# A decoder trunk on one core: the maximum of a weight strip over the partitions, by GpSimd's all-reduce or by two transfers through DRAM and a VectorE maximum

## The chip, the cores and the metric

The kernel runs on one core of one Trainium2 chip. The metric is the device time of one execution in microseconds. The kernel before was run three times, and its median is the number to compare with.

A core has a matrix engine (TensorE, PE in the profile, with its weight loads as PEld), VectorE (DVE), ScalarE (ACT), GpSimd (POOL) and a sync engine (SP), which in this kernel does nothing but issue transfers. Each engine works through its own queue in order. An instruction whose inputs are not there yet holds up all that stands behind it in that queue, and nothing in the others.

## What is computed

The reference is one inference step of a small hybrid decoder: 1,024 prompt tokens with 16 meta tokens ahead of them, and 8 single new tokens of running sequences, 1,048 columns in all, with a model width of 1,024. Cut to what matters:

```python
for i in range(2):
    h = rms_norm(x, norm_mix_pre[i])
    m = ssd_mixer(h, ...) if i == 0 else rglru_mixer(h, ...)
    x = x + rms_norm(m, norm_mix_post[i])
    h = rms_norm(x, norm_ffn_pre[i])
    r = relu(h @ ffn_w1[i])                                  # 1024 -> 4096
    x = x + rms_norm((r * r) @ ffn_w2[i], norm_ffn_post[i])  # 4096 -> 1024
```

Inputs and weights are float32. The mixers have products with weights too: 1024 to 6176 and 2048 to 1024 in the first (SSD), 1024 to 2048 and 1024 to 1024 in the second (LRU).

## The kernel before

**Weights in strips.** Every product with weights is made from float16 parts: a float32 operand is scaled by a power of two and split into a high and a low part, and three products (high by high, high by low, low by high) are summed in PSUM. The weights come in strips of [128, 8 x 256] float32, 1 MB each. `wlane` (line 399) walks through the list of strips that `setup` made (lines 216 to 232). For each it starts the load of the next one on SP (`load_strip`, line 257, into one of two buffers `ws`), and converts the present one (`wconv`, line 285) into float16 tiles `wh`, of which there are five. The steps of a conversion are:

- the largest magnitude in each partition, [128, 1], called `rm`: a VectorE reduction for most kinds of strip (for the ffn's second product by way of `r4`, `r4s`), an ACT sum of magnitudes as a bound for the SSD strips (kind a), or a number that was found earlier (`gmx`, kind s);
- `strip_scale` (line 262): the maximum of `rm` over the 128 partitions, on every partition (`wgb`), by `partition_all_reduce` on GpSimd; then tiny VectorE steps, in the trace `qw`, `pw`, `sw`, `winv`, that make a power of two of it (`pow2`, line 245);
- for strips of kinds H and S, `quarter` and `sums` (lines 340 and 349): three quarters of the strip are split into `wp` by ACT and VectorE, then four GpSimd instructions add and subtract quarters within the strip (`ws<-ws`), for Winograd's form of the product (seven quarter products for eight);
- `split` (line 271): the high parts by ACT, the low parts by VectorE, into `wh`. When the last is done, the strip's buffer is free for a load.

There are 109 strips with a scale of their own: 33 in the SSD layer (of which one is a narrow one for dt), 32 in each of the two ffns, 12 in the LRU layer. Two more all-reduces are made once each: of the gains at the start (`gb`, line 191) and of bounds in the LRU layer (`gx`, line 1487).

**The ffn.** `ffn` (line 1226) makes four blocks, each with four strips of the first product and four of the second. In the blocks after the first (and, for the second product, in the first three) a unit of 256 rows by a chunk of some 350 tokens is computed by `unit` (line 1350): matmuls into four PSUM tiles, and VectorE and ACT steps that empty them into a tile `z`. GpSimd makes the sums of quarters of the right operand: for the squares in `t_sums` (line 1319, tiles `z` and `r`), and for the ffn's input, while the first block's second product runs, in `input_sums` (line 1332, tiles `f`). ACT and VectorE then split these into float16 (`TT`, `HT`, `H`). The tiles `z`, `r` and `f` share four buffers.

**Other transfers near the change.** In the SSD layer SP loads cumulative sums spread over the partitions for each chunk of 128 tokens (`L<-csd`, line 1017, two buffers), and sends one small row per group through DRAM and back, spread over all partitions (`bcd<-row`, line 1090, and `bc<-bcd`, line 1093).

**What sets the order.** The conversion of strips, the norms and the sums are generators; `tick` (line 127) takes one step of each between products. This sets a priority. The framework then orders the instructions of each engine by priority and by when it reckons their inputs to be there, so an engine's order is not just that of the program: the `qw` of a strip can stand ahead of the `wh` of the strip before. It also sets the semaphores that every instruction waits for. Nearly all instructions are issued through one helper, so that the profile gives them line 89 (or 92, inside a block with a forced order); they are told apart by the names of their tiles.

Tiny tiles come from the pool `tiny` (line 156) with three buffers per name, unless said otherwise.

Of the kernel before, what the change touches and what calls it, by code (L numbers as in the profile page):

```python
# [21 lines left out]
P = 128  # L22
# [31 lines left out]
def cols(c):  # L54
    """The columns of a chunk of tokens."""
    return slice(c * CW, c * CW + WC[c])


class Carve:
    """Small float32 tiles cut from larger ones."""  # L60
# [17 lines left out]
class Queue:  # L78
    """An engine; while hold is set its instructions are issued in program order, and later ones behind them."""
# [38 lines left out]
class Body:  # L118
# [7 lines left out]
    # ------------------------------------------------------- order of work  # L126
    def tick(self):
        """One step of every piece of work that runs beside the matrix products."""
        for lane in list(self.lanes):
            if next(lane, self) is self:  # L130
                self.lanes.remove(lane)
# [5 lines left out]
    def tab(self, *args, **kw):  # L137
        """An activation whose function needs a table set: these stay in program order."""
        if self.last_tab is None or self.nc.scalar.hold:
            self.last_tab = self.nc.scalar.activation(*args, **kw)  # L140
        else:
            with self.tc.issue_after(self.last_tab.ins):
                self.last_tab = self.nc.scalar.activation(*args, **kw)
# [8 lines left out]
    # ---------------------------------------------------------------- setup  # L152
    def setup(self):
        nc, tc, ctx = self.nc, self.tc, self.ctx
        self.const = ctx.enter_context(tc.tile_pool(name="const", bufs=1))
        self.tiny = ctx.enter_context(tc.tile_pool(name="tiny", bufs=3))
# [25 lines left out]
        # pre-norm gains and group-norm gains scaled by a power of two so that hi/lo fit float16  # L182
# [13 lines left out]
        # the inputs of the ffn leave room for sums of four  # L196
# [13 lines left out]
        self.csd = self.dram.tile([288, P], F32, name="csd")  # L210
        self.bcd = [self.dram.tile([8, 2, P], F32, name=f"bcd{i}") for i in range(2)]
# [33 lines left out]
    def pow2(self, b, n, pool, tag):  # L245
        """p = the power of two at or below b; s = 2^14 / p."""
# [9 lines left out]
    # -------------------------------------------------------------- weights  # L256
# [5 lines left out]
    def strip_scale(self, gmax):  # L262
        nc, ty = self.nc, self.tiny
        gb = ty.tile([P, 1], F32, tag="wgb", name="wgb")
        nc.gpsimd.partition_all_reduce(gb, gmax, P, RED.absmax)
        s, p = self.pow2(gb, 1, ty, "w")
        inv = ty.tile([P, 1], F32, tag="winv", name="winv", bufs=8)
        nc.vector.tensor_scalar(inv, p, 2.0 ** -14, None, op0=OP.mult)
        return s, inv, gb

    def split(self, w, st, s, parts):
        """w = float16 hi and lo parts of st * s, s [P, parts] by contiguous column ranges."""
# [12 lines left out]
    def wconv(self, st, kind, cols=SW):  # L285
        """A strip of weights as float16 hi and lo parts [P, 2, KT, cols], the factor that undoes its scaling and,
        for kinds h and H, the factor of its hidden units. Kind a takes a bound from the sums of the magnitudes, kind s
        one that kind g found before; kinds 2 and S carry the factors of the hidden rows. Kinds H and S are for the
        products by Winograd's form: with the quarters that are used as they are."""
# [50 lines left out]
    def quarter(self, s, inv):  # L340
        """Scales that leave room for sums of four."""
# [7 lines left out]
    def sums(self, wp, st, s, npair, parts):  # L349
        """Steps: the quarters of a strip [K tiles, M] that are used as they are, A11, A12, A22 (A ij: m tile i, k  # L350
        tiles of parity j), as float16 parts in wp; then the sums of Winograd's form in the room of the strip. Only
        the first npair pairs of k tiles."""
# [20 lines left out]
    def product(self, ps, i, w, B, T, npair):  # L373
        """ps = one of the seven products of quarters over the first pairs of k tiles, three passes of the float16
        parts; open for the products of the other pairs where there are any."""
# [14 lines left out]
    def quadrant(self, w, B, npair, i, l):  # L390
        """The operands of m tile i by half l of the tokens over the other pairs."""
# [26 lines left out]
    def hidden_scale(self, wmax, inv):  # L418
        """The factors of one strip's hidden units: t = 2^7, or 2^6 where the squares are summed, / (power of two at or
        below the bound on the values before the square, the norm of the input times that of a column); returns  # L420
        t / (scales of the product); 1 / t^2 goes to rj."""
# [21 lines left out]
    def summed(self, b, s):  # L443
        """Whether the hidden units of a strip of block b enter the second product by Winograd's form."""
        return b < 3 and s < NSUM
# [6 lines left out]
    def bundle(self, ps, w, m, act, c, kts=range(KT), first=True, last=True):  # L452
        """ps += sum over k of w[k, m tile]^T act[k, chunk c], three passes of the float16 parts."""
# [14 lines left out]
    def new_u(self):  # L468
        """Float16 parts of the normed input by chunk and k tile."""
# [4 lines left out]
    def u_rows(self, U, c):  # L474
        """The bytes of chunk c of U as float32 rows."""
        return U[:, c].bitcast(F32).rearrange("p k s c -> p k (s c)")

    # ---------------------------------------------------------------- norms
    def rstd(self, sumsq, n, pool, w):
        """1 / sqrt(mean + eps) on every partition, from per-partition sums of squares."""  # L480
# [17 lines left out]
    def normed(self, x, ss, i, hi, lo, pool):  # L498
        """Steps: the pre-norm i of a chunk (its k tiles in x), as float16 parts in hi and lo [P, KT, n]."""
# [15 lines left out]
    def boundary(self, m, ss, xc, piece, ipost, xdst, ipre, U, pool):  # L515
        """Steps: x + norm(m) for a piece of a chunk to xdst; then its pre-norm."""
# [37 lines left out]
    def last_phase(self, ws, act, ipost, xsrc, xdst, ipre, evac, pre=None, split0=None):  # L554
        """The last product before a norm, chunk by chunk; the norms of a chunk run beside the next one."""
# [47 lines left out]
    def first_phase(self, strips, act, evac):  # L603
        """Products of the first strips after a norm: chunk 2 of the input comes last."""
# [15 lines left out]
    # ------------------------------------------------------------------ SSD  # L620
# [67 lines left out]
    def start_x(self, c):  # L688
        """A chunk of the input, in the room of later rows: its k tiles, and room left over."""
# [25 lines left out]
    def start_norm(self, U, c, x, sq, ufs):  # L715
        """Steps: the first pre-norm of a chunk."""
# [29 lines left out]
    def start(self, U):  # L746
        """The first pre-norm beside the first products, issued in this order."""
# [20 lines left out]
    def dt_phase(self, U, dts, dtt, w):  # L768
        """Step sizes, decays and their cumulative sums, tokens on partitions: columns (tile, head); tiles 0-7
        are the chunks of the prompt, 8 the meta tokens, 9 the sample tokens."""  # L770
# [31 lines left out]
        # the sums again, tokens along the rows, in DRAM, from where they are spread over the partitions  # L802
# [22 lines left out]
        # sample tokens  # L825
# [3 lines left out]
        # head rows by sample, then spread over the partitions of the features  # L829
# [13 lines left out]
    def softplus(self, out, x, pool, n, parts=1):  # L843
        """max(x, 0) + log1p(exp(-|x|)), the logarithm by the series of 2 artanh(e / (2 + e)); by parts of the
        columns that don't wait for each other."""
# [23 lines left out]
    def evac_ext(self, pre, ps, c, inv, bias=0.0):  # L869
        """A chunk of projected columns into the layout of the convolution: 8 x (3 state + 1), 3 zeros, tokens."""  # L870
# [10 lines left out]
    def conv_tile(self, pre, out, w4, b1, cvo):  # L881
        """Depthwise convolution of width 4; the last three columns of each sequence go to cvo [P, 27]."""
# [16 lines left out]
    def proj_x(self, g, start=False):  # L899
        """Projection and convolution of the x, B and C columns of a group."""  # L900
# [84 lines left out]
    def ssd_group(self, g):  # L985
# [26 lines left out]
        def spread(i):  # L1012
            """The cumulative sums of a chunk's tokens on every partition."""
# [68 lines left out]
        def sample_bc():  # L1082
            """B and C of the sample tokens, by way of DRAM, on every partition."""
# [22 lines left out]
        def sample_b(b2):  # L1106
            """Two sample tokens: h += x B and y = h C, B and C spread over the partitions."""
# [45 lines left out]
    def group_norm(self, g):  # L1153
        """Steps: gate, norm within the group, float16 parts."""
# [25 lines left out]
    def half_a(self):  # L1180
        """The first half of the output projection, kept in DRAM by chunks."""
# [43 lines left out]
    # ------------------------------------------------------------------ FFN  # L1225
    def ffn(self, l):
# [8 lines left out]
        for b in range(4):  # L1235
# [3 lines left out]
            def square(c, s, r):  # L1239
                """The squares of r (m tile, half of the tokens) as float16 parts, and their sums."""  # L1240
# [78 lines left out]
    def t_sums(self, f, t1, t234):  # L1319
        """Steps: the sums of quarters of the right operand for Winograd's form, in their room in f (B jl: k tiles of  # L1320
        parity j, half l of a chunk's tokens, the last half first): T1 = B12 - B11, T2 = B22 - T1, T3 = B22 - B12,
        T4 = B21 - T2, and their float16 parts."""
# [9 lines left out]
    def input_sums(self, U, TT, fp):  # L1332
        """Steps: the sums of quarters of the input, T1 in the room of B12 and the others in TT."""
# [16 lines left out]
    def unit(self, w, BT, c, npair, fp):  # L1350
        """Two m tiles by a chunk, [C12, C11, C22, C21] (C il: m tile i, half l of the tokens, the last half first), the
        first pairs of k tiles by Winograd's form: seven products of quarters."""
# [27 lines left out]
    # ------------------------------------------------------------------ LRU  # L1380
    def lru(self):
# [99 lines left out]
        # a bound on |h gate|: (32.3 max|x| + max|h0|) (norm of u times that of a column of weights + max|b|)  # L1481
# [74 lines left out]
def _strips(w, ns):  # L1556
    """[K, N] as [ns, 128, (K / 128) * (N / ns)], each strip contiguous per partition."""
# [4 lines left out]
def _fm(x):  # L1562
    """[..., n * 128] as [128, n, ...]"""
# [95 lines left out]
```

## Time and profile before

| | |
|---|---|
| runs | 2830.25, 2836.51, 2837.24 us |
| median | 2836.51 us |
| profiled execution, span | 2836.7 us |
| VectorE, ACT busy | 2110.1 us (74%), 1322.6 us (47%) |
| mean granted TensorE clock | 0.968 |
| all-reduces of strips on GpSimd | 109 (100 + 5 + 4 in three groups) |

A line of a group of instructions gives line, engine, operation, the tiles (written <- read), the shapes and the count; then busy time in us and the mean in ns of one; then the idle time of that engine just before these instructions and what ended most of it ("issue" means nothing that the profile shows). A timeline row gives start and duration in us, the instruction and how many were merged, and in brackets the engine's idle time before the first of them. SPq, POOLq are an engine's sequencer, that waits and issues transfers. A row of DMA issues ends with the size in KB and the median time from issue to landing in us. The SSD layer fills the time to about 900 us, its last product and norm reach to about 1060, the first ffn to about 1690, the LRU layer to about 2110, the second ffn to the end.

### The profile page before, as it was taken

The page shows a single profiled execution, that of the slowest core. Times are in us where ns is not written, and L with a number is a line of the kernel's source. Part 1 is how long each engine was busy: PE and PEld are TensorE (multiplying, and loading weights), DVE is VectorE, ACT ScalarE, POOL GpSimd, SP SyncE. Part 2 cuts the span into 40 slices and gives each one's busy share as a digit, 9 for nine tenths or more (in the row PEclk, how much of TensorE's full clock was granted, in tenths as well). Part 3 has the DMA queues.
Part 4 walks back from the last instruction along what each step waited for, and adds up shares of the span by engine and source line. Part 5 has one row for each costly group of instructions (what it writes and reads, how often), then busy time and mean ns, then how long its engine had stood idle before and what let it go on. Part 6 is the DMA issues. An engine that isn't in the chain of part 4 may idle for free. (4 is left out here: it accounts for less than half of the span.)

```text
span 2836.7 us, 56933 instructions
## 1 busy us (share of the span) xinstructions
PE 2583.1 (91%) x23209; PEld 2060.6 (73%) x23209; DVE 2110.1 (74%) x5043; ACT 1322.6 (47%) x2148; POOL 691.4 (24%) x972
## 2 busy tenths in 40 slices
PE   4999999999999999789989999979999779989998
PEld 2666666666666667789989976646667779989976
DVE  4889778977873685568778788787685667878776
ACT  4655455545544354344253344658564335253352
POOL 2222111212212024442232201123014452231301
PEclk9999999999999999889999999989999989999999
DMA  3232233223345320101122123110220101111122
GB/s 123 99 119 90 87 107 115 102 88 108 113 159 187 117 106 31 46 31 46 61 72 79 46 110 113 63 62 33 89 108 31 46 31 46 47 45 53 54 73 95
DMA packets 52758, 229.15 MB, mean 81 GB/s; under 512 B 9056, under 2 KB 18416, under 8 KB 31632
## 3 DMA queue, kind: packets, MB, share of 16 engines
q1 hardware_dynamic: 46112, 190.81, 19.1%
q0 software_dynamic: 6384, 34.71, 3.1%
q8 instruction: 181, 2.97, 0.4%
q14 instruction: 81, 0.66, 0.1%
HBM read 186.28 MB, written 39.22 MB: 79 GB/s over the span
## 5 line engine op out<-in xcount | busy, mean ns | idle before, releaser
L89 PEld LDWEIGHTS <-wh 128*128 128x128 f16 x17040 | 1504.0, 99 | 503.7 <-issue 54.7
L89 PE MATMUL mm<-U,wh 128*128 128x350 f16 (+3 forms) x7056 | 989.4, 297 | 20.7 <-ACT rr L89 13.2
L89 PE MATMUL mm<-H,wh 128*128 128x175 f16 (+5 forms) x5664 | 557.7, 253 | 35.3 <-DVE z L89 30.4
L89 PEld LDWEIGHTS <-wp 128*128 128x128 f16 x3888 | 311.0, 99 | 87.6 <-issue 60.5
L89 POOL TENSOR_TENSOR ws<-ws 128x256 f32<-128x256 f32 (+1 forms) x192 | 205.2, 1069 | 328.6 <-DVE wp L89 214.4
L89 DVE TENSOR_TENSOR z<-z,mm 128x175 f32<-128x175 f32 (+3 forms) x648 | 228.4, 370 | 29.2 <-ACT z L89 22.0
L89 POOL PARTITION_ALL_REDUCE wgb<-rm x100 | 55.5, 555 | 656.6 <-issue 338.4
L89 PE MATMUL mm<-U,wp 128*128 128x175 f16 (+1 forms) x1728 | 154.8, 245 | 55.2 <-DVE z L89 55.1
L89 PE MATMUL mm<-TT,wh 128*128 128x175 f16 (+1 forms) x1728 | 167.0, 248 | 10.2 <-ACT TT L89 9.3
L89 ACT ACTIVATE z<-z,ti 128x700 f32<-128x700 f32 (+1 forms) x72 | 63.0, 875 | 183.5 <-DVE z L89 183.5
L89 DVE SCALAR_TENSOR_TENSOR wh<-ws,sw,wh 128x1024 f16<-128x1024 f32 x94 | 122.0, 1320 | 28.3 <-ACT wh L89 28.3
L89 DVE TENSOR_SCALAR qw<-wgb 128x1 f32<-128x1 f32 x103 | 15.5, 150 | 167.3 <-POOL wgb L89 167.1
L89 DVE SCALAR_TENSOR_TENSOR wh<-ws,s,wh 128x256 f16<-128x256 f32 x256 | 114.7, 490 | 11.1 <-ACT wh L89 11.1
L89 DVE TENSOR_REDUCE rm<-ws 128x1 f32<-128x2048 f32 x40 | 91.3, 2281 | 31.2 <-DMA ws<-w 26.7
L89 PE MATMUL mm<-H,wp 128*128 128x175 f16 (+1 forms) x864 | 90.5, 241 | 25.5 <-DVE z L89 23.1
L89 DVE TENSOR_TENSOR ss<-ss,sqt 128x350 f32<-128x350 f32 (+3 forms) x154 | 75.9, 500 | 41.8 <-ACT sqt L89 41.1
L89 ACT ACTIVATE wh<-ws,s 128x512 f16<-128x512 f32 x128 | 83.0, 710 | 48.0 <-POOL ws L89 23.2
L89 DVE SCALAR_TENSOR_TENSOR conv<-pre,ssmall,conv 128x1072 f32<-128x1072 f32 x78 | 103.8, 1330 | 0.1
L89 ACT ACTIVATE wh<-ws,sw 128x2048 f16<-128x2048 f32 x47 | 93.7, 1993 | 14.5 <-DVE sw L89 11.7
L89 DVE TENSOR_SCALAR L<-L,ncs 128x128 f32<-128x128 f32 (+1 forms) x288 | 90.6, 357 | 13.2 <-DMA L<-csd 13.2
L89 DVE TENSOR_TENSOR H<-z,H 128x175 f16<-128x175 f32 (+5 forms) x120 | 81.2, 694 | 23.6 <-ACT H L89 19.5
L89 ACT ACTIVATE pre<-mm,undo 128x8 f32<-128x8 f32 (+1 forms) x104 | 46.5, 474 | 110.7 <-PE mm L89 110.7
(279 smaller groups left out, 4176.9 us busy)
## 6 DMA issues: line engine op xcount, KB each, us to landing
ws<-w SPq DMA_DIRECT2D x64, 1024.0 KB, 4.9
ws<-w_ssd_in SPq DMA_DIRECT2D x24, 1024.0 KB, 5.4
L<-csd SPq DMA_DIRECT2D x64, 256.0 KB, 3.2
ws<-w_lru_in SPq DMA_DIRECT2D x12, 1024.0 KB, 4.9
xd<-xc POOLq DMA_DIRECT2D x6, 1400.0 KB, 5.5
xc<-xd SPq DMA_DIRECT2D x6, 1400.0 KB, 6.0
h<-ssd_h SPq DMA_DIRECT2D x8, 1024.0 KB, 4.9
bc<-bcd SPq DMA_DIRECT2D x8, 1024.0 KB, 4.8
```

What stands on the lines that cost most here:

```text
L89: r = f(*args, **kw)
```

## The change

`strip_scale` no longer uses GpSimd. The 128 maxima are written to a small DRAM tile (one of four in turn) by SP; SP then reads this tile as a row of 128 numbers onto each of the 128 partitions (the tile `wrow`, one buffer), and VectorE takes the maximum of the row. The pool `tiny` has two buffers per name instead of three. The rest of the diff takes out docstrings and comments; the two other all-reduces stay.

```diff
-        self.tiny = ctx.enter_context(tc.tile_pool(name="tiny", bufs=3))
+        self.tiny = ctx.enter_context(tc.tile_pool(name="tiny", bufs=2))
...
         self.csd = self.dram.tile([288, P], F32, name="csd")
+        self.mxd = [self.dram.tile([P, 1], F32, name=f"mxd{i}") for i in range(4)]
+        self.nmax = 0
...
     def strip_scale(self, gmax):
         nc, ty = self.nc, self.tiny
+        d = self.mxd[self.nmax % 4]
+        self.nmax += 1
+        nc.sync.dma_start(d, gmax)
+        row = ty.tile([P, P], F32, tag="wrow", name="wrow", bufs=1)
+        nc.sync.dma_start(row, d.rearrange("p o -> o p").to_broadcast([P, P]))
         gb = ty.tile([P, 1], F32, tag="wgb", name="wgb")
-        nc.gpsimd.partition_all_reduce(gb, gmax, P, RED.absmax)
+        nc.vector.tensor_reduce(gb, row, axis=AX.X, op=OP.max)
         s, p = self.pow2(gb, 1, ty, "w")
```

## The prediction

> **What bounds the kernel now.** I read the page first, then TensorE's groups, then the stages one by one, and then what TensorE waits for.
>
> ```profile
> span 2836.7 us, 56933 instructions
> PE 2583.1 (91%) x23209; PEld 2060.6 (73%) x23209; DVE 2110.1 (74%) x5043; ACT 1322.6 (47%) x2148; POOL 691.4 (24%) x972
> ```
>
> The profiled execution takes 2836.7 us, the median of the runs is 2836.51, so sums made on the span need no correction. TensorE is busy 91%: only its idle time, 254 us, and a slower clock can be won. On the busy row GpSimd (POOL) looks harmless with 24%.
>
> ```profile
> L89 PE MATMUL mm<-H,wh 128*128 128x175 f16 (+5 forms) x5664 | 557.7, 253 | 35.3 <-DVE z L89 30.4 <-DVE H L89 2.8 <-DVE sw L89 1.5
> L89 PE MATMUL mm<-U,wp 128*128 128x175 f16 (+1 forms) x1728 | 154.8, 245 | 55.2 <-DVE z L89 55.1
> L89 PE MATMUL mm<-H,wp 128*128 128x175 f16 (+1 forms) x864 | 90.5, 241 | 25.5 <-DVE z L89 23.1 <-DVE iq L89 1.8 <-DVE sq L89 0.5
> ```
>
> These three groups are the ffn's Winograd products; 116 us of idle time stand before them, nearly all ended by VectorE's z, the emptying of PSUM. VectorE itself is idle a quarter of the time, so the question is what holds z up. By stage (columns: PE, PEld, DVE, ACT and POOL busy, granted clock, DMA share, GB/s):
>
> ```profile
> 100.00:900.00 800.00, 762.51 (x5074) 533.41 (x5073) 632.16 (x1729) 407.20 (x620) 169.71 (x280) 0.98 0.32 113
> 1060.00:1150.00 90.00, 82.72 (x820) 69.98 (x818) 51.59 (x127) 40.00 (x82) 37.81 (x59) 0.96 0.10 36
> 1150.00:1300.00 150.00, 119.09 (x1357) 116.05 (x1355) 95.78 (x240) 62.33 (x103) 67.89 (x94) 0.87 0.10 36
> 1300.00:1690.00 390.00, 362.57 (x4473) 347.73 (x4471) 313.36 (x774) 156.30 (x268) 88.02 (x104) 0.98 0.20 73
> 2110.00:2220.00 110.00, 103.12 (x959) 82.79 (x958) 63.93 (x153) 51.31 (x103) 43.74 (x70) 0.97 0.09 30
> 2220.00:2340.00 120.00, 90.21 (x1046) 87.13 (x1044) 73.68 (x183) 44.69 (x73) 58.72 (x79) 0.87 0.10 36
> 2340.00:2740.00 400.00, 369.83 (x4669) 362.20 (x4667) 312.27 (x794) 164.36 (x288) 95.73 (x118) 0.98 0.15 54
> ```
>
> The loss sits in the ffn: six stages with 132 us of TensorE idle (stretch less PE busy), worst at 1150 to 1300 and 2220 to 2340. Those two have the lowest clock as well. Now the engines around one large gap; first GpSimd, then TensorE, then VectorE:
>
> ```profile
> 2484.50 5.38 POOL L89 TENSOR_TENSOR ws<-ws 128x512 f32<-128x512 f32 x4 [9.19 <-issue]
> 2496.07 0.41 POOL L89 PARTITION_ALL_REDUCE wgb<-rm  x1 [6.19 <-issue]
> 2503.60 4.00 POOL L89 TENSOR_TENSOR z<-z 128x175 f32<-128x175 f32 x8 [7.12 <-DVE wp L89]
> ```
> ```profile
> 2497.46 1.08 PE L89 MATMUL mm<-U,wp 128*128 128x175 f16 x12 [1.58 <-DVE z L89]
> 2510.39 1.90 PE L89 MATMUL mm<-U,wp 128*128 128x174 f16 x12 [6.07 <-DVE z L89]
> ```
> ```profile
> 2485.97 2.29 DVE L89 TENSOR_REDUCE rm<-ws 128x1 f32<-128x2048 f32 x1 [0.94 <-DMA ws<-w]
> 2496.51 0.15 DVE L89 TENSOR_SCALAR qw<-wgb 128x1 f32<-128x1 f32 x1 [4.58 <-POOL wgb L89]
> ```
>
> The strip's maxima (rm) are there at 2488.26, and the all-reduce itself takes 0.41 us. But GpSimd stands still for 6.19 us before it, having ended its sums at 2489.88, and for 7.12 us after it. Of the 63 places in this trace where the all-reduce follows a TENSOR_TENSOR directly, and the 63 the other way round, these are the ones with the least idle time:
>
> ```profile
> 1069.58 0.41 POOL L89 PARTITION_ALL_REDUCE wgb<-rm  x1 [5.74 <-issue]
> 1251.08 4.18 POOL L89 TENSOR_TENSOR z<-z 128x175 f32<-128x175 f32 x8 [6.69 <-DVE wh L89]
> ```
>
> Never less, while the eight sums of the second row ran without a gap among them. I call this the swap, some 13 us a pair; it is counted in no busy time. It costs twice. VectorE, whose queue is in order, stands at qw for 4.58 us, and TensorE loses 1.58. Then GpSimd's sums z come late, the ACT and VectorE steps behind them too, and TensorE loses 6.07.
>
> ```profile
> 2504.30:2509.50 5.20, 0.02 (x1) 0.00 (x0) 2.46 (x5) 2.67 (x7) 3.30 (x7) 1.00 0.43 176
> 2509.50:2516.30 6.80, 5.91 (x42) 5.91 (x42) 5.38 (x13) 2.05 (x5) 4.82 (x6) 0.50 0.01 4
> ```
>
> After the gap the granted clock is 0.50 for 6.8 us: a long gap is paid a second time, by 3.4 us here.
>
> **What is removed.** 109 all-reduces in the strips (two others, gb and gx, stay) and with them nearly all swaps: the swap lies between the two kinds of operation, and only the elementwise kind is left.
>
> ```profile
> L89 POOL PARTITION_ALL_REDUCE wgb<-rm x6 | 2.5, 411 | 35.9 <-issue 30.1 <-DVE z L89 5.9
> L89 DVE TENSOR_SCALAR qw<-wgb 128x1 f32<-128x1 f32 x20 | 3.1, 154 | 56.2 <-POOL wgb L89 56.2
> ```
>
> The first row is the stretch 1150 to 1300: six all-reduces with 35.9 us of standstill before them; at 6.7 at least for the way back another 40, so that GpSimd's 67.89 us of work and 76 us of swaps fill the 150. There GpSimd is the bound behind z. Without swaps it has half the stretch free. The second row is 2340 to 2740: VectorE stands 56.2 us before 20 strips, 2.8 each.
>
> **What is added.** Per strip a write of 128 x 4 bytes, a wait for its landing in SP's queue, a broadcast read of 64 KB, and a VectorE maximum of 128 elements. No such pair of transfers for a strip is in the trace; the nearest is the row that the SSD stage sends through DRAM and back (bcd, bc), then single small transfers:
>
> ```profile
> 128.64 0.34 SPq L1090 DMA_DIRECT2D bcd<-row  x1
> 132.22 0.35 SPq L907 DMA_DIRECT2D cst<-ssd_cst  x1
> 132.66 0.38 SPq L1093 DMA_DIRECT2D bc<-bcd  x1
> ```
> ```profile
> 201.70 0.30 SPq L1090 DMA_DIRECT2D bcd<-row  x1
> 203.55 0.33 SPq L1093 DMA_DIRECT2D bc<-bcd  x1
> ```
> ```profile
> ws<-w SPq DMA_DIRECT2D x64, 1024.0 KB, 4.9
> ws<-w_dt SPq DMA_DIRECT2D x1, 128.0 KB, 2.1
> lru_h_o<-lhout POOLq DMA_DIRECT2D x1, 36.0 KB, 2.0
> ```
> ```profile
> L89 DVE TENSOR_REDUCE rm<-ws 128x1 f32<-128x2048 f32 x40 | 91.3, 2281 | 31.2 <-DMA ws<-w 26.7 <-DMA ws<-w_lru_out 2.5 <-DMA ws<-w_lru_in 1.8
> L89 DVE TENSOR_REDUCE r<-ws 128x2 f32<-128x1024 f32 x64 | 76.1, 1210 | 13.3 <-DMA ws<-w 13.3
> ```
>
> Write to read issue: 1.85 us at 201.70, 4.02 at 128.64; I take 1.85, since the first had another transfer's issue between. Read: 2.1 as for 128 KB. Maximum: (2281 - 1210) / 1024 = 1.05 ns an element, so 139 + 134 = 273 ns. Sum 4.2 us from rm to the strip's maximum. Bounds: 4.0 (two transfers at the 2.0 of the smallest) and 4.02 + 4.9 + 2.1 + 0.3 = 11.3, when a strip's load of 1 MB is in the queue ahead of the read. The old way took 8.2 us at 2488.26 (to 2496.48), and only 0.5 where no swap is needed. The Trainium skill (DMA: Bandwidth & Descriptors, Specifications) speaks against the write: under 512 B a transfer is done as read-modify-write. No row here has pieces of 4 bytes; the 288-byte pieces of lhout landed in 2.0 us. By an estimate from that page's shortest HBM round trip, 0.8 us (its section on latency), the rule would add at most 64 x 0.8 = 51 us over the ffn's strips.
>
> Two more effects. VectorE gets 109 x 0.27 = 30 us of work; in the ffn stages it is idle at least a fifth of the time, so I cost it at nothing there; without that cover it is 64 x 0.27 = 17 us. The tiny tiles go from three buffers to two, also at nothing: a strip's scale is read within the strip, and the next one but one has no place to be loaded (two buffers for strips) before the first is split; if that cover fails, a strip's scale waits about a strip, and the end is as in the second rival.
>
> SP's queue is new on the path. What stands in it:
>
> ```profile
> SPq L259 <- DVE wh L89: 1659.7, 97, 66.2
> ```
>
> 97 strip loads waited there for the split of an older strip, 17 us each. So SP is mostly free when rm comes, and the write goes at once; but behind the read's wait (1.85 us) stand L's loads in the SSD stage and the loads of x at the ends of the layers, and behind both VectorE.
>
> **The sum.** (a) 1150 to 1300 and 2220 to 2340: idle 30.9 + 29.8, half clock 0.13 x 270 = 35, together 96; GpSimd gets half its time back; 70% goes, since its real work, and ACT's and VectorE's steps behind it, still come in bursts: -67. (b) 1300 to 1690 and 2340 to 2740: idle 27.4 + 30.2, clock 0.02 x 790 = 16, together 73; half goes, as VectorE's wait falls from 2.8 us but not to zero: -37. (How far it falls hangs on the order of VectorE's queue, which the framework makes anew. It does not keep the order of the program: it may lay other work into the 4.2 us, or none.) (c) 1060 to 1150 and 2110 to 2220: 14 idle and 7 clock, little of it behind strips: -4. (d) The start: the first two strips' transfers queue behind the inputs, but the next gap shrinks:
>
> ```profile
> 34.47 0.41 POOL L92 PARTITION_ALL_REDUCE wgb<-rm  x1 [5.79 <-issue]
> 41.66 6.68 POOL L92 TENSOR_TENSOR ss<-ss,sq 128x350 f32<-128x350 f32 x7 [6.78 <-issue]
> ```
>
> 6.78 us of that swap stand before sums that TensorE waits for; against it up to 7 us for the first strip: -4. (e) SSD stage: VectorE is 79% busy and gets 24 x 0.27 = 6.5 us, SP's waits come on top, some swaps go: +3. (f) New waits at the maximum, 50 strips of 0.15 us past what TensorE tolerates: +8. Sum -101, so 2736. What is late next is z behind ACT and TensorE's own pace.
>
> **Rivals.** First, nothing is won: the standstill belongs to GpSimd's sums and would stand before them anyway, or VectorE's own work is next at once. For it: VectorE is 78% busy in (b). Against: sums follow sums without a gap, and (a) has VectorE at 64%. Time 2836, within 0.3% (8.5 us, about what a measurement of this kernel tells from no change).
>
> Second, slower: the read of the maxima lands behind a 1 MB load in SP's queue. The place is qw: VectorE, in order, stands there, and z behind it. TensorE tolerates 3.0 us of this (4.58 less the 1.58 it lost). A wait of 5.5 gives a gap of 2.5, and at least 1.7 more by the clock, in 64 strips: 269; less the (a) of 67 it is +202, 3039. It decides from a wait of 3.0 + 67 / 64 = 4.0 us. For it: 11.3 us is possible by rows. Against: loads go out only after a split, and the read needs only 2 us.
>
> Third, dear transfers: the op was cheap (0.41) and two transfers take 3.8 us more; if the swaps were hidden anyway and all of this showed in 64 strips, 243 us more, 3080. The Trainium skill (GPSIMD Engine Reference, 4.1 Engine selection) is on its side: reduce along partitions on GpSimd. The rows with 6.19 and 7.12 us around 0.41 speak against.
>
> Fourth, nearly everything goes: 190 us of (a) to (c) less the 50 that no swap explains, and the start: under 2690.
>
> **Numbers.** Forecast 2736 with 0.77 in 2690 to 2805 (low: 90% of (a), 75% of (b), 10 at the start; high: 40% of (a), nothing of (b)); 0.04 between that and 2828; no change 0.05; second rival 0.04; third 0.02; fourth 0.08. Faster by over 0.3% 0.89, same 0.05, slower 0.06.
>
> **What would show it.** In the changed profile: GpSimd's sums without 6 us before them; the 1150 to 1300 stretch shorter, its clock near 1; VectorE's idle before qw or the new maximum under 1 us a strip; write to read about 1.9 us. Wrong: over 3 us of idle time before the maximum, z still late with GpSimd free, or new waits at L in the SSD stage.

## The result: 3309 us, slower by a sixth

| | median of the runs | lowest to highest |
|---|---|---|
| before | 2833.55 us (4 runs: the three above and one more) | 2830.25 to 2837.24 |
| changed | 3308.69 us (4 runs) | 3303.52 to 3313.22 |

The ratio is 1.167, with a 95% interval of 1.165 to 1.169. The profiled execution of the changed kernel has a span of 3301.8 us, 465.1 more than before. First the busy row of its page:

```profile
PE 2693.6 (82%) x23209; PEld 2146.5 (65%) x23209; DVE 2125.7 (64%) x5152; ACT 1317.6 (40%) x2148; POOL 649.3 (20%) x863
```

No engine has much more to do: VectorE 16 us, GpSimd 42 less. TensorE is idle for 608 us instead of 254, and its own 2693.6 us are 110 more for the same 23,209 matmuls, with a mean granted clock of 0.913 where it was 0.968. So work waits. To see where, I cut the span at the places where TensorE has done as many matmuls as at the stage borders of the prediction. The columns are those of the prediction's stage rows:

```profile
108.90:985.10 876.20, 785.81 (x5075) 545.89 (x5073) 653.10 (x1796) 414.15 (x631) 158.61 (x256) 0.95 0.35 104
1281.60:1448.50 166.90, 118.90 (x1357) 115.52 (x1355) 96.31 (x251) 62.46 (x106) 61.48 (x82) 0.87 0.10 35
1448.50:1948.10 499.60, 392.46 (x4473) 379.53 (x4472) 306.97 (x765) 149.37 (x259) 79.14 (x84) 0.88 0.16 55
1948.10:2439.90 491.80, 406.86 (x2505) 261.57 (x2504) 343.17 (x579) 257.25 (x380) 68.72 (x73) 0.92 0.25 74
2672.60:3202.50 529.90, 400.70 (x4670) 393.41 (x4668) 313.32 (x802) 164.46 (x286) 85.27 (x97) 0.87 0.13 41
```

The third and fifth rows, stage (b) of the prediction, took 790 us before and take 1029.5 now: half of the loss. The SSD stage (first row) loses 76 and the LRU layer (fourth row) 72; a table further down has all stages. What TensorE waits for (us in total, times, longest), its two largest waits now and its largest before:

```profile
PE mm L89 <- DVE z L89: 225.2, 71, 9.0
PE mm L89 <- DVE pw L89: 88.8, 18, 6.4
```
```profile
PE mm L89 <- DVE z L89: 113.2, 70, 6.2
```

It hardly ever waits for a strip's parts: for `wh` less than 4 us in the whole run. Both z, the emptying of PSUM, and pw stand on VectorE, and there mostly behind one instruction, the new maximum. Its group, the DMA issues of the two transfers (count, KB, median us from issue to landing), and SP's waits (us in total, times, longest), for a strip's load and between the two transfers:

```profile
L89 DVE TENSOR_REDUCE wgb<-wrow 128x1 f32<-128x128 f32 x103 | 29.3, 284 | 710.6 <-DMA wrow<-mxd 710.6
```
```profile
wrow<-mxd SPq DMA_DIRECT2D x109, 64.0 KB, 4.9
mxd<-rm SPq DMA_DIRECT2D x105, 0.5 KB, 8.3
```
```profile
SPq L261 <- DVE wh L89: 905.9, 88, 29.4
SPq L271 <- DMA mxd<-rm: 749.9, 95, 14.1
```

The maximum itself takes 284 ns, as priced at 273. But VectorE stands 710.6 us in front of 103 of them, 6.9 each, because the write of 512 bytes lands after 8.3 us and the read, which goes only then, after 4.9 more. (These are medians of the landings that the profile can place, about a quarter of them. By the issues of all strips it is 8.4 us from write to read and 5.0 from the read to the maximum.) One strip of the second ffn, first SP's queue, then three VectorE rows, then TensorE:

```profile
3017.66 0.33 SPq L261 DMA_DIRECT2D ws<-w  x1
3025.68 0.32 SPq L269 DMA_DIRECT2D mxd<-rm  x1
3034.69 0.32 SPq L271 DMA_DIRECT2D wrow<-mxd  x1
3047.57 0.33 SPq L261 DMA_DIRECT2D ws<-w  x1
```
```profile
3023.37 2.29 DVE L89 TENSOR_REDUCE rm<-ws 128x1 f32<-128x2048 f32 x1 [2.05 <-DMA ws<-w]
...
3039.37 0.29 DVE L89 TENSOR_REDUCE wgb<-wrow 128x1 f32<-128x128 f32 x1 [10.57 <-DMA wrow<-mxd]
...
3046.94 0.48 DVE L89 SCALAR_TENSOR_TENSOR wh<-ws,s,wh 128x256 f16<-128x256 f32 x1
```
```profile
3040.56 1.06 PE L89 MATMUL mm<-H,wh 128*128 128x175 f16 x6 [6.41 <-DVE pw L89]
```

Read this as a loop. The load issued at 3017.66 lands 5.71 us later, its row maxima take 2.29, the route through DRAM 13.71 (3025.66 to 3039.37), and 8.20 after that the next load goes. That load was waiting for a buffer, and the buffer for the last low part of the strip before (the row at 3046.94), and that work stands in VectorE's queue behind the wait for the row. The four steps add up to 29.91 us a strip, and nothing of one overlaps another. TensorE stands 6.41 us beside it, since z waits behind the maximum.

### The profile page after: what moved, and what is told of

The parts are those of the page before. It is cut to its first block, busy times and chain, and to the rows that moved or that the text cites. A ratio compares the mean times of both kernels' runs of the same rounds, so it can differ in the third digit from the quotient of the medians.

```text
span 3301.8 us, 57041 instructions
## 1 busy us (share of the span) xinstructions
PE 2693.6 (82%) x23209; PEld 2146.5 (65%) x23209; DVE 2125.7 (64%) x5152; ACT 1317.6 (40%) x2148; POOL 649.3 (20%) x863
## 5 line engine op out<-in xcount | busy, mean ns | idle before, releaser
L89 PEld LDWEIGHTS <-wh 128*128 128x128 f16 x17040 | 1566.5, 102 | 676.5 <-issue 116.2
L89 PE MATMUL mm<-U,wh 128*128 128x350 f16 (+3 forms) x7056 | 1016.1, 301 | 97.3 <-DVE z L89 24.8
L89 PE MATMUL mm<-H,wh 128*128 128x175 f16 (+5 forms) x5664 | 585.8, 261 | 99.5 <-DVE pw L89 61.7
L89 DVE TENSOR_REDUCE wgb<-wrow 128x1 f32<-128x128 f32 x103 | 29.3, 284 | 710.6 <-DMA wrow<-mxd 710.6
L89 PEld LDWEIGHTS <-wp 128*128 128x128 f16 x3888 | 325.2, 102 | 185.8 <-issue 183.5
L89 PE MATMUL mm<-TT,wh 128*128 128x175 f16 (+1 forms) x1728 | 178.7, 259 | 0.0
L89 ACT ACTIVATE wp<-ws,sq 128x512 f16<-128x512 f32 x72 | 48.5, 711 | 156.0 <-issue 63.5
L89 ACT ACTIVATE wp<-ws,s 128x128 f16<-128x128 f32 x144 | 48.2, 389 | 152.3 <-issue 86.2
L89 ACT ACTIVATE H<-z 128x700 f16<-128x700 f32 (+1 forms) x96 | 64.7, 674 | 102.3 <-POOL z L89 100.7
L89 PE MATMUL mm<-Y,wh 128*128 128x350 f16 (+1 forms) x576 | 93.9, 326 | 10.1 <-ACT Y L89 7.3
```

The source lines that it names most:

```text
L89: r = f(*args, **kw)
```

## The experiments

The main theory (A): the price is how the bytes lie in DRAM. 128 pieces of 4 bytes side by side make the write's landing late, and 128 partitions that read the same 512 bytes make the read late. Its rival (B): a pair of transfers through DRAM costs this here however they lie, by SP's queue and the loads of 1 MB. Beside these stands the question whether the gain that I forecast, from GpSimd's swaps, exists at all.

**Side by side or apart, the same row or one's own.** Three kernels, each with four DRAM tiles of [128, 128], filled with 64 at the start. The write's pieces lie side by side or 512 bytes apart; every partition reads the same 512 bytes, or a row of its own. Apart and own rows:

```diff
-        self.mxd = [self.dram.tile([P, 1], F32, name=f"mxd{i}") for i in range(4)]
+        self.mxd = [self.dram.tile([P, P], F32, name=f"mxd{i}") for i in range(4)]
...
-        nc.sync.dma_start(d, gmax)
+        nc.sync.dma_start(d[:, 0:1], gmax)
...
-        nc.sync.dma_start(row, d.rearrange("p o -> o p").to_broadcast([P, P]))
+        nc.sync.dma_start(row, d)
```

Side by side, own rows: 

> The transfers as in the changed kernel, but each partition reads a 512-byte row of its own from a 64 KB tile in DRAM; the write still puts its 128 pieces of 4 bytes next to each other. The rows hold a constant but for the first, so the maximum is not the one over the partitions (it is taken with the partition's own). Theory A (128 reads of the same 512 bytes are what makes the read slow): issue to landing of the read falls from 4.9 to about 2.1 us, the write's stays at 8.3, time about 3308 - 109 x 2.8 x 0.75 = 3080. Theory B (the read is slow because it comes right after a slow write, whatever it reads): the read stays at 4.9 and the time near 3300.

Apart, the same row: 

> The write puts its 128 pieces of 4 bytes 512 bytes apart; all partitions still read one and the same 512 bytes (of which one number is a maximum, so the scale is not that over the partitions). Theory A (pieces of 4 bytes that fall into one stretch of DRAM hold each other up): issue to landing of the write falls from 8.3 to about 2 us, the read's stays at 4.9, time about 3308 - 64 x 6.3 - some of the other strips, so 2850 to 2900. Theory B (a piece of 4 bytes is slow wherever it goes): the write stays at 8 us, time near 3300.

Apart, own rows: 

> Both: the pieces of the write 512 bytes apart, and each partition reads a row of its own (so the maximum is the partition's own or a constant). Theory A: write about 2 us, read about 2.1, the round trip 4.2 as predicted; then the rest of the prediction is put to the test: 2736, or 2690 to 2805. Theory B: the route stays above 10 us and the time above 3200.

One run each, beside one of the kernel before at 2843.03 us. The waits in the last column are those ahead of the maximum on VectorE:

| write | read | time | write lands | read lands | waits |
|---|---|---|---|---|---|
| side by side | same 512 B (the change) | 3308.69 us | 8.3 us | 4.9 us | 710.6 us |
| side by side | own rows | 3148.67 us | | | 559.1 us |
| 512 B apart | same 512 B | 2706.84 us | 1.4 us | 2.8 us | 106.2 us |
| 512 B apart | own rows | 2685.40 us | 1.4 us | 1.7 us | 52.7 us |

For the second line the profile has no landing times; in its timeline the read's issue comes 7.8 us after the write's (8.4 in the change) and the maximum 3.7 after that (5.0), as medians of all strips. This kernel has one more small step on VectorE per strip, against the partition's own maximum. The DMA issues of the third line, and the maximum in the fourth:

```profile
wrow<-mxd SPq DMA_DIRECT2D x109, 64.0 KB, 2.8
mxd<-rm SPq DMA_DIRECT2D x105, 0.5 KB, 1.4
```
```profile
L89 DVE TENSOR_REDUCE wgb<-wrow 128x1 f32<-128x128 f32 x103 | 28.9, 281 | 52.7 <-DMA wrow<-mxd 52.1
```

The same number of transfers, bytes and pieces through the same queue: A holds and B falls, as they are put above; the second line, between its two forecasts, shows that own rows alone mend little while the write is slow. Laying the pieces apart takes 602 us from the time, own rows 160 with the slow write and 21 with the fast one (single runs, so the last is rough). The times of the two kernels with pieces apart were not hit: 2850 to 2900 was expected with the same row, where the read was to stay at 4.9 us, and at least 2690 with own rows; both are faster. The read of the same row is 1.1 us slower than that of own rows (2.8 against 1.7); why it takes another 2.1 behind the slow write stays open.

**How far apart.** The same own-row reads; the pieces of strip after strip lie 4, 8, 16, 64, 128 and 512 bytes apart in turn (tiles pa to pf).

```diff
+        self.mxd = [(self.dram.tile([P, P], F32, name=n), w) for n, w in
+                    (("pa", 1), ("pb", 2), ("pc", 4), ("pd", 16), ("pe", 32), ("pf", 128))]
...
+        nc.sync.dma_start(d.rearrange("a b -> (a b)")[:P * w].rearrange("(p w) -> p w", w=w)[:, 0:1], gmax)
```

> The read takes each partition's own row, as before; the write's pieces of 4 B lie 4, 8, 16, 64, 128 or 512 B apart (tiles pa to pf), strip by strip in turn, so that one kernel shows six receipts. The scale is not the strip's maximum (rows hold 64s and maxima of other strips). Theory A, the receipt grows with the pieces that share 512 B (128, 64, 32, 8, 4, 1; 0.05 us a piece): from write to the read's issue 7.7, 4.6, 3.0, 1.8, 1.6 and 1.5 us. Rival (pieces that share 512 B at all are dear): five of the six at 5 to 8 us, only 512 B at 1.5.

One run, 2780.99 us. Its DMA issues, and one pair of issues on SP in the second ffn:

```profile
pa<-rm SPq DMA_DIRECT2D x18, 0.5 KB, 7.3
pb<-rm SPq DMA_DIRECT2D x18, 0.5 KB, 3.2
pc<-rm SPq DMA_DIRECT2D x18, 0.5 KB, 1.9
pd<-rm SPq DMA_DIRECT2D x17, 0.5 KB, 1.4
pe<-rm SPq DMA_DIRECT2D x17, 0.5 KB, 2.8
pf<-rm SPq DMA_DIRECT2D x17, 0.5 KB, 1.4
```
```profile
2260.17 0.32 SPq L274 DMA_DIRECT2D pe<-rm  x1
2261.62 0.32 SPq L276 DMA_DIRECT2D wrow<-pe  x1
```

The price falls faster than I expected: 7.3, 3.2 and 1.9 us at 4, 8 and 16 bytes where one price for each piece gives 7.7, 4.6 and 3.0, and nothing is left at 64. (The profile can place only three to seven landings of each tile. From the write's to the read's issue the middle strip of the two ffns took 7.5, 3.1 and 1.9 us at 4, 8 and 16 bytes, and 1.45 at each of the other three.) The 2.8 at 128 bytes, from four landings, is not the distance: in the SSD stage, where SP has other loads between the two issues, four of these writes took 9.9 to 14.3 us to the read's issue; of nine in the ffn the middle one takes 1.45, as in the two rows. So the rival (any sharing of 512 bytes is dear) falls too, and my one price per piece with it: only the direction was right. The reads, all of own rows, follow the write before them: 3.2, 2.7, 2.2 and 1.8 us to their landing at 4, 8, 16 and 64 bytes. So a read that comes behind a slow write is slow itself; why, no run shows.

**Four pieces instead of 128.** VectorE turns the column by blocks of 32 x 32, and four rows of 128 bytes fill the same 512 bytes of DRAM. The read is the change's own.

```diff
+        t32 = ty.tile([P, 32], F32, tag="wt32", name="t32", bufs=1)
+        nc.vector.transpose(t32, gmax.to_broadcast([P, 32]))
-        nc.sync.dma_start(d, gmax)
+        nc.sync.dma_start(d, t32[0:P:32, :])
```

> The change with its write in four pieces of 128 B: VectorE turns the column by 32 x 32 blocks (about 0.1 us), rows 0, 32, 64 and 96 go to the same 512 B of DRAM, and the read is the change's own. Computes what the reference asks. Theory A, by the number of pieces in one stretch: (7.75 - 1.48) / 127 = 0.05 us a piece, so the write takes about 1.6 us to the read's issue, the read 2.8 as with pieces apart, and the time is 2700 to 2730. Rival (any piece of under 512 B that shares its stretch with another one is dear): the write takes 5 us or more, 2950 to 3300.

2733.13 us (2725.12 to 2739.10, 4 runs), ratio to before 0.965 (0.963 to 0.967): a gain, and 576 us under the change. One strip, on SP and on VectorE:

```profile
2484.61 0.50 SPq L271 DMA_DIRECT2D mxd<-t  x1
2486.21 0.32 SPq L273 DMA_DIRECT2D wrow<-mxd  x1
```
```profile
2484.19 0.15 DVE L89 TENSOR_REDUCE rm<-r4s 128x1 f32<-128x4 f32 x1
2484.38 0.21 DVE L89 STREAM_TRANSPOSE t<-rm 128x32 f32<-128x32 f32 x1
...
2489.04 0.28 DVE L89 TENSOR_REDUCE wgb<-wrow 128x1 f32<-128x128 f32 x1 [1.71 <-DMA wrow<-mxd]
```

The read goes 1.60 us after the write, and rm to maximum takes 4.70 us where the change takes 13.71. With a turn of 0.21 us on VectorE on top, this is the kernel that my prediction described, and the stages can be held against its terms:

```profile
1126.10:1253.10 127.00, 109.46 (x1358) 106.28 (x1356) 93.22 (x250) 60.63 (x101) 58.66 (x80) 0.97 0.13 46
1253.10:1626.40 373.30, 356.89 (x4473) 343.76 (x4471) 313.97 (x804) 154.14 (x267) 79.14 (x84) 1.00 0.21 74
...
2152.80:2244.70 91.90, 82.61 (x1045) 80.83 (x1043) 69.28 (x172) 38.95 (x65) 48.07 (x63) 0.98 0.14 49
2244.70:2626.20 381.50, 361.80 (x4669) 354.85 (x4667) 314.55 (x821) 164.32 (x287) 86.47 (x98) 1.00 0.17 57
```

| stage (us, equal TensorE work) | before | changed | four pieces |
|---|---|---|---|
| SSD layer, 100 to 900 | 800 | 876.2 | 792.9 |
| its last product, 900 to 1060 | 160 | 193.1 | 159.9 |
| (c) of the prediction | 200 | 217.4 | 179.5 |
| (a) | 270 | 285.6 | 218.9 |
| (b) | 790 | 1029.5 | 754.8 |
| LRU layer, 1690 to 2110 | 420 | 491.8 | 425.9 |
| start and end | 196.7 | 208.2 | 191.4 |
| span | 2836.7 | 3301.8 | 2723.3 |

**What the swaps cost.** Two kernels without the route. In the first each partition takes its own row maximum; the second adds to it an all-reduce whose result nobody reads.

```diff
-        nc.gpsimd.partition_all_reduce(gb, gmax, P, RED.absmax)
+        nc.vector.tensor_copy(gb, gmax)
...
+        un = ty.tile([P, 1], F32, tag="unread", name="unread")
+        nc.gpsimd.partition_all_reduce(un, gmax, P, RED.absmax)
```

> Leaves out the maximum over the partitions: each partition takes its own row maximum (one copy on VectorE in the all-reduce's place), so the scales are not the strip's; no transfer and no all-reduce. The kernel before otherwise, with its three buffers per small tile. Theory A (GpSimd's alternation of all-reduces and elementwise work costs the kernel before its 100 us and more; the route costs what is left): at or under the 2685 us of the kernel with pieces apart and own rows, 2640 to 2690. Theory B (the gain of the kernels with pieces apart came from something else in the change, the buffers or the order): 2800 to 2836.

> As the kernel without a maximum over the partitions, and the all-reduce is issued where it was, into a tile that nobody reads: GpSimd's alternation is back, VectorE's wait for its result is not. Theory A1 (the standstill of GpSimd itself delays the pieces that GpSimd prepares): most of the gain is lost, 2780 to 2836. Rival A2 (the strip's wait for the result of the all-reduce was the cost): within 20 us of the kernel without a maximum, some 2670.

2676.08 us (ratio 0.945, 0.943 to 0.947) and 2800.39 us (0.989, 0.988 to 0.991). So of the 156 us between the kernel before (2832.29 in these rounds) and one without any maximum over the partitions, 124 come back with an all-reduce that no other engine waits for; the other 32 are left for the wait for its result. GpSimd in the second kernel:

```profile
2420.36 5.85 POOL L89 TENSOR_TENSOR ws<-ws 128x512 f32<-128x512 f32 x4 [8.97 <-DVE wp L89]
2432.07 0.41 POOL L89 PARTITION_ALL_REDUCE unread<-rm  x1 [5.86 <-issue]
2440.17 5.85 POOL L89 TENSOR_TENSOR ws<-ws 128x512 f32<-128x512 f32 x4 [7.70 <-DVE wp L89]
2451.86 0.41 POOL L89 PARTITION_ALL_REDUCE unread<-rm  x1 [5.84 <-DVE z L89]
```

The standstills are there with nobody waiting: 5.86 and 5.84 us before an all-reduce that follows sums, though its input (rm) was there at 2425.03 and 2444.66, before the sums ended. A1 holds.

**VectorE's order alone.** The changed kernel with its slow transfers, but the maximum is put behind the split of the strip before.

```diff
-        nc.vector.tensor_reduce(gb, row, axis=AX.X, op=OP.max)
+        if self.lo is None:
+            nc.vector.tensor_reduce(gb, row, axis=AX.X, op=OP.max)
+        else:
+            with self.tc.issue_after(self.lo.ins):
+                nc.vector.tensor_reduce(gb, row, axis=AX.X, op=OP.max)
```

> The changed kernel with its slow transfers, and VectorE's order alone changed: the maximum of a strip's row is put behind the split of the strip before. Computes what the reference asks. Theory L (the loop: the next load waits for that split, and that split stands behind the wait for the row, so load 5.7, row maxima 2.3, route 13.7 and split 8.2 come one after the other, 29.9 us a strip): the loop is cut, some 8 us of split fill the wait, and the time falls to 2750 to 2900. Rival V (what costs is VectorE standing still with z behind it; the load's loop costs little): the wait is still about 7 us a strip, over the 3.0 that TensorE bears, and the time stays at 3100 or above.

3015.36 us (ratio 1.064, 1.062 to 1.066). The maximum, and SP's queue over two strips:

```profile
L89 DVE TENSOR_REDUCE wgb<-wrow 128x1 f32<-128x128 f32 x103 | 29.0, 281 | 346.0 <-DMA wrow<-mxd 346.0
```
```profile
2792.79 0.32 SPq L270 DMA_DIRECT2D mxd<-rm  x1
2800.48 0.32 SPq L272 DMA_DIRECT2D wrow<-mxd  x1
2802.58 0.33 SPq L262 DMA_DIRECT2D ws<-w  x1
2815.62 0.32 SPq L270 DMA_DIRECT2D mxd<-rm  x1
```

The next load now goes 2.10 us after the read's issue, not 12.88, and the strips follow each other at 22.83 us. That gives back 293 of the 475 us that the change lost; the transfers are as slow as ever (7.69 us from write to read), and 3.4 us of VectorE's wait are left for each strip. Neither figure was hit: L forecast at most 2900, V at least 3100. The new order shortens two things at once, SP's wait to load the next strip (905.9 us in the change, 473.1 here) and VectorE's wait at the maximum (710.6 and 346.0). So the 293 us are what the order is worth; how much of them is the loop and how much VectorE's standing this run does not tell.

The same order in the kernel with four pieces:

> The same order in the kernel with four pieces of 128 B. Computes what the reference asks. Theory L: the route of about 4.7 us is mostly covered by the split; 2690 to 2733. Rival: the maximum comes later than it could, the strip's pieces are late at TensorE, 2740 to 2780.

2716.27 us (ratio 0.959, 0.957 to 0.960), with 36.0 us ahead of the maximum instead of 135.8: L's side, and the shortest time of the kernels here that scale a strip by its own maximum.

**Without DRAM and without GpSimd.** TensorE turns the column, spread to 128, into PSUM, where VectorE takes the maximum.

```diff
+        ps = self.mm()[:, :P]
+        nc.tensor.transpose(ps, gmax.to_broadcast([P, P]), self.ident)
...
+        nc.vector.tensor_reduce(gb, ps, axis=AX.X, op=OP.max)
```

> The maximum over the partitions without GpSimd and without DRAM: TensorE turns the column, spread to 128 columns, into PSUM, and VectorE takes the maximum of each row from there. Computes what the reference asks. Theory A (what counts is the length of the route; VectorE waits for one small product of TensorE): under 2 us of route, 2650 to 2720. Rival (the small product stands in TensorE's order ahead of products that were ready, and TensorE waits at it for VectorE, which is some microseconds behind): 109 waits of about 3 us and the clock with them, 3000 or more.

2923.06 us (ratio 1.033, 1.031 to 1.035): the hoped-for route failed, and not quite as the rival had it. What TensorE waited for (us in total, times, longest), then one strip on VectorE and TensorE:

```profile
PE mm L89 <- ACT wh L89: 99.8, 36, 6.7
PE mm L89 <- DVE wh L89: 67.9, 82, 1.9
...
PE mm L89 <- DVE rm L89: 12.0, 6, 4.7
```
```profile
2392.28 0.16 DVE L89 TENSOR_REDUCE rm<-r4s 128x1 f32<-128x4 f32 x1
...
2412.65 0.28 DVE L89 TENSOR_REDUCE wgb<-mm 128x1 f32<-128x128 f32 x1
```
```profile
2411.27 0.27 PE L89 MATMUL mm<-ident,rm 128*128 128x128 f32 x1
```

At the small product itself it stands 12.0 us in all. It is the other way round: the maximum waits its turn in TensorE's order. After the rm of 2392.28 the next such product runs at 2411.27, and the strip's parts (wh) then come late, 167.7 us of waits.

**Two buffers.** The change's other edit alone, in the kernel before.

```diff
-        self.tiny = ctx.enter_context(tc.tile_pool(name="tiny", bufs=3))
+        self.tiny = ctx.enter_context(tc.tile_pool(name="tiny", bufs=2))
```

> The kernel before with two buffers for each small tile in place of three, the change's other edit alone. All theories of the route: no difference over 0.3 %. Rival (the scale's small tiles come free too late with two buffers): slower by 0.5 % or more, and then part of the change's loss is this.

2836.27 us, ratio 1.0014 (1.0000 to 1.0027): within 0.3%, no part of the loss.

## Why the prediction was wrong

**The step that failed** is the price of the route: "Write to read issue: 1.85 us at 201.70, 4.02 at 128.64; I take 1.85" and "Read: 2.1 as for 128 KB", sum 4.2, bound 11.3. Measured 8.3 and 4.9, and 13.7 from rm to maximum. The rows I took were near in kind (single small transfers) and in bytes, and far in the one thing that counts: the row that the SSD stage writes has 8 KB on 8 partitions, lhout has 288 bytes on each partition, the new write 4 bytes, side by side. The upper bound came from the same rows with a load ahead, so it could not hold this either. I did see that "No row here has pieces of 4 bytes" and then bounded their price by 64 shortest round trips, 51 us "at most", though a shortest trip bounds nothing from above.

**The terms of the sum**, with the route at its forecast length (the four pieces, 4.7 us), came out near in all:

| term | forecast | four pieces |
|---|---|---|
| (a) swaps, worst stages | -67 | -51 |
| (b) swaps, other ffn stages | -37 | -35 |
| (c) | -4 | -20.5 |
| (d) start | -4 | -5 (start and end) |
| (e) SSD | +3 | -7 |
| all | -101 | -113 |

So 2733.13 stands where 2736 was forecast. (The column is the profiled execution, the fastest of the four; by the medians the gain is 99 us.) The reason for the gain was right; that the sum is so near is partly luck, since (a) gave 16 us less than forecast and (c), nearly left out, 16.5 more. The kernel without any maximum shows that 57 us more were in reach. (f) was to be 8 us of new waits in places not named; the LRU layer's +6 is the only one of that sign.

**The second rival was the right picture with the wrong cause.** VectorE stands at the maximum, z behind it, from a wait of 4.0 us on; the wait is 6.9, and 9.3 in the two stages of (b) (343.9 us before 37 maxima). Its cause is no load in the queue but the write's landing. Its price, 3039, is too low, because it was worked out for a wait of 5.5 us and for the ffn's 64 strips alone: the ffn's stages lose 272.5 us against its 202, and 181 us of the loss lie in the SSD layer, its last product and the LRU layer. What it did not see is the loop, which keeps the route from being covered: the load waits for a split that stands behind the wait. I had written down both halves, the buffers ("has no place to be loaded ... before the first is split") and the order ("does not keep the order of the program"), and not joined them; the other order in VectorE's queue is worth 293 us, by the loop and the shorter wait together. The first rival (nothing won) did not come about. The fourth (under 2690) is where the kernels with pieces apart and own rows (2685.40) and without a maximum (2676.08) stand, not the change. The third, dear transfers, was right about the sign, and the swaps were not hidden.

**At nothing, and rightly so:** VectorE's work of 0.28 us a strip (the kernel with pieces apart and own rows has it, and with its transfers is 9 us above the one without any maximum), the two buffers (2836.27), SP's queue in the SSD stage (792.9 for 800 with the short write).

The Trainium skill's advice (GPSIMD Engine Reference, 4.1 Engine selection) to reduce along partitions on GpSimd is met here by 124 us for the alternation of two kinds of work on it; the two transfers beat it when the write is laid out well, and lose to it when it is not.

## What to carry to other kernels

Price a small transfer by its pieces and how they lie, not by its bytes: when no row of the trace has pieces of that size lying that way, the cost is unknown, and one look at such a write alone is worth more than a bound from its neighbours. When a wait is put into an in-order queue, follow the buffers as well: ask whether what stands behind the wait is what frees the next load, since then the wait lies in a loop that the next strip's load cannot cover. An operation that is cheap on its own engine may still be dear by what it does to the operations before and after it.

## What the hardware showed that I had not expected

A write of 128 pieces of 4 bytes lands after 7.3 to 8.3 us when the pieces are side by side, 3.2 at 8 bytes apart, 1.9 at 16 and 1.4 at 64 and at 512. The time is not in the queue. In the changed kernel, SP's two issues of one strip of the LRU layer:

```profile
2054.28 0.33 SPq L269 DMA_DIRECT2D mxd<-rm  x1
2062.36 0.33 SPq L271 DMA_DIRECT2D wrow<-mxd  x1
```

The DMA engines' records in this trace show the last 4-byte packet of this write ended 1.02 us after its issue; SP got the word 8.08 us after it. With the pieces 512 bytes apart the last 4-byte packet ended 1.02 us after the issue as well (the middle write of all strips), and the write landed after 1.4. The Trainium skill (DMA: Bandwidth & Descriptors, Anatomy of one DMA) puts most of a transfer's fixed 2 us into the receipt of the write by its target, told there for transfers that GpSimd issues. The place agrees, since some 7 us here lie behind the last packet; the size does not. The same page's rule on pieces under 512 bytes (Specifications) does not tell the two layouts apart: pieces of 4 bytes that lie 64 bytes apart land in 1.4 us. Why near neighbours cost this much no run here shows.
